# Sliding attention: two masked score blocks merged ahead of the exponent and parted behind the transpose

## The chip, the cores and the metric

The kernel runs on one NeuronCore of a Trainium2 chip. Its time is device microseconds of one execution; three runs were timed. The engines are named as in the profile: PE is TensorE's matmul, PEld its weight load, DVE is VectorE, ACT is ScalarE, POOL is GpSimd, SP is SyncE, which issues most DMAs.

## The reference

Two layers of a hybrid decoder over 256 tokens of width 1024, in float32. Each layer normalises its input, projects it once into everything that three parallel mixers need (a state-space scan called SSD, sliding-window attention, forgetting attention called fox), gates and projects the three results, merges them and adds the sum to the residual. The change lies in the sliding-window attention, 16 heads in 4 groups that share keys and values:

```python
qb = q.reshape(b, nb, blk, SWA_KV_HEADS, SWA_GROUP, HEAD_DIM)      # blk = 128, nb = 2
scores = jnp.einsum('bnqkgd,bnskd->bnkgqs', qb, kb) * (HEAD_DIM ** -0.5)
diff = qi + blk - sj                                               # sj: 0..255, own block and the one before
band = (diff >= 0) & (diff < SWA_WINDOW)                           # window 128
scores = jnp.where(mask, scores, -jnp.inf)
probs = jax.nn.softmax(jnp.concatenate([scores, sink], axis=-1), axis=-1)[..., :-1]
out = jnp.einsum('bnkgqs,bnskd->bnqkgd', probs, vb)
return out * jax.nn.silu(z)
```

The window is as long as a block. A query of the second block at place i sees the keys of its own block at places j <= i, and those of the block before at places j > i. So of the two keys with the same place j, one in each block, it sees exactly one. A query of the first block has only its own block.

## The kernel before, in words

The work is a long row of dense products on TensorE: the input projection in pieces of 256 or 512 columns, then the branch projections and the output projection. Weights come in by DMA (`raw`, issued by SyncE), ScalarE copies them to a rounded high part (`hi`, L264) and VectorE subtracts that from them for a low part (`lo`, L265). Each product takes three passes over the high and low parts (`dense`, 24 matmuls for one unit). Up to six `hi` and `lo` tiles are held.

TensorE executes in the order in which the program is written out (`tc.manual_schedule(engines={ENG.PE})`). The order on VectorE, ScalarE and GpSimd is made by the framework's scheduler from the dependences; each engine then executes its own list in order.

Small work is put between the dense products by a planner. It keeps a clock in estimated TensorE microseconds (`mm` and `transpose` add to it). A piece of small work is a generator. When it yields a number, such as `D_SOFT = 7.0`, `D_SOFT2 = 3.0` or `D_EVAC = 3.0`, it may go on at the first call of `pump` after so much of that clock; when it yields a function, it waits until that is true; when it yields the name of a token, it waits for the token. `pump` is called at the end of a dense unit, and in the middle of one with 512 columns, and enters what is due, earliest first, until 1.35 of the clock is used up. `drain` forces all work of one branch to its end ahead of the projection that needs it.

A *quad* is the attention of four query heads, in two pairs p of two heads i. `swa_quad` makes the four quads of the sliding attention in each layer, `fox_quad` the four of the forgetting attention; both run the common `attn_quad` (L528). With the one `pp` token it

- scores both query blocks b of each head (8 matmuls into 4 PSUM tiles of the 5 named `mx`): block 0 against 128 keys, block 1 against 256;
- adds the mask or bias, scales by -1/8 and takes the row minimum on VectorE (L555), into `pp`, where a head has 128 columns for block 0 and 256 for block 1;
- takes the exponent with its row sum on ScalarE (L561), adds the sink's term to the sum (L565 to L568), and multiplies by half the reciprocal on VectorE (L573, 8 per quad; the half belongs to the SiLU of the gate);
- `D_SOFT` later, transposes the three 128 by 128 blocks of each head on TensorE (L100), 12 per quad in two blocks of six that `D_SOFT2` parts; ScalarE copies each four of them to SBUF (L590);
- `D_EVAC` later, gives the token back and, when the gate is there, multiplies with the values (8 matmuls, L96, `mx<-L,L`) and with the gate on VectorE (L603).

The sliding quads run beside the projections of the gate (`u_z`), of the convolution (`u_conv`) and the values of fox (`u_cv`). The SSD groups (`ssd_group`) begin when no work of the sliding branch waits any more. GpSimd prepares the biases of the fox quads (`affine_select`, L867), adds the rotated halves of queries and keys (L492, L513) and little else. In `u_bkv`, ScalarE copies the values from PSUM to `y.bv`.

## Time and profile before

| | us |
|---|---|
| three runs: lowest, median, highest | 847.7, 848.38, 850.29 |
| span of the profiled execution, from its first to its last instruction | 846.0 |
| PE busy | 833.7 |
| PEld busy | 763.4 |
| DVE busy | 642.3 |
| ACT busy | 511.6 |
| POOL busy | 105.7 |

The page gives the profiled execution by its span; what lies around the span is not in it, and the median of the timed runs is 2.4 us above it. Busy time of an engine is the union of its instructions' spans; matmuls overlap, so the sum of their durations is larger than the busy time. In the lists of groups, a line gives the line of the kernel, engine, operation, tiles written and read, shapes and count, then the group's busy time in us and the mean duration of one in ns, then the idle time of the engine just before such instructions and what ended it. A row of the timeline gives start and length in us, then the same names. A row of the windows gives a stretch and the busy time and count of instructions of each engine in it, then the TensorE clock granted (1.00 is full), the share of the DMA engines, and GB/s. The row of one line's instructions gives the shortest, median and longest duration in ns.

### The profile page before, as it was taken

The page shows a single profiled execution, that of the slowest core. Times are in us where ns is not written, and L with a number is a line of the kernel's source. Part 1 is how long each engine was busy: PE and PEld are TensorE (multiplying, and loading weights), DVE is VectorE, ACT ScalarE, POOL GpSimd, SP SyncE. Part 2 cuts the span into 40 slices and gives each one's busy share as a digit, 9 for nine tenths or more (in the row PEclk, how much of TensorE's full clock was granted, in tenths as well). Part 3 has the DMA queues.
Part 4 walks back from the last instruction along what each step waited for, and adds up shares of the span by engine and source line. Part 5 has one row for each costly group of instructions (what it writes and reads, how often), then busy time and mean ns, then how long its engine had stood idle before and what let it go on. Part 6 is the DMA issues. An engine that isn't in the chain of part 4 may idle for free.

```text
span 846.0 us, 15985 instructions
## 1 busy us (share of the span) xinstructions
PE 833.7 (99%) x5964; PEld 763.4 (90%) x5964; DVE 642.3 (76%) x1403; ACT 511.6 (60%) x1004; POOL 105.7 (12%) x134
## 2 busy tenths in 40 slices
PE   8999999999999999999999999999999999999996
PEld 7989898998999998888989998899899999988896
DVE  5777997998776669656788879879968567785665
ACT  6466777665666667435555667776557667654442
POOL 6410100000140010210014001000003110121000
PEclk9999999999999999999999999999999999999999
DMA  9576565666465545748676465465755654576632
GB/s 303 160 226 197 180 199 163 197 212 184 143 188 177 181 145 189 230 147 292 206 237 218 144 204 157 145 200 182 239 172 176 174 175 152 161 236 211 212 100 76
DMA packets 126638, 158.43 MB, mean 187 GB/s; under 512 B 12784, under 2 KB 88224, under 8 KB 126560
## 3 DMA queue, kind: packets, MB, share of 16 engines
q1 hardware_dynamic: 109456, 140.79, 52.5%
q10 hardware_dynamic: 17056, 16.49, 6.3%
q8 instruction: 47, 0.77, 0.4%
q14 instruction: 31, 0.25, 0.1%
q0 software_dynamic: 48, 0.13, 0.0%
HBM read 155.22 MB, written 2.16 MB: 186 GB/s over the span
## 4 chain that ended last, share of the span: by engine, by line
PE 95%; DMA 3%; DVE 1%; ACT 0%; POOL 0%; issue 0%; SPq 0%; POOLq 0%; DVEq 0%
PE mm L96 82%; PE mx L96 9%; PE mx L100 4%; DMA raw<-in_w_in_dram 3%; DVE lo L265 0%; POOL lo L1154 0%; ACT hi L1153 0%; DVE L L470 0%; ACT L L1013 0%; DVE L L265 0%; ACT L L264 0%; POOLq L1218 0%; ACT L L215 0%; DVE L L996 0%; DVE L L1001 0%
## 5 line engine op out<-in xcount | busy, mean ns | idle before, releaser
L265 DVE TENSOR_TENSOR lo<-raw,hi 128x1024 fp32r<-128x1024 f32 x252 | 308.3, 1235 | 93.8 <-ACT hi L264 84.6
L96 PE MATMUL mm<-hi,L 128*128 128x512 f32 (+1 forms) x1344 | 373.9, 364 | 2.0 <-ACT hi L1153 1.5
L264 ACT ACTIVATE hi<-raw 128x1024 fp32r<-128x1024 f32 x252 | 263.4, 1056 | 93.5 <-PE mm L96 75.5
L96 PE MATMUL mm<-L,hi 128*128 128x256 f32 x1792 | 317.7, 278 | 0.7 <-DVE L L473 0.7
L96 PEld LDWEIGHTS mm<-L,hi 128*128 128x128 f32 x1792 | 277.7, 192 | 7.6 <-issue 3.3
L96 PEld LDWEIGHTS mm<-hi,L 128*128 128x128 f32 x1344 | 241.5, 190 | 32.5 <-issue 2.7
L96 PE MATMUL mm<-L,lo 128*128 128x256 f32 x896 | 246.4, 275 | 0.0
L96 PE MATMUL mm<-lo,L 128*128 128x512 f32 (+1 forms) x672 | 241.4, 361 | 0.6 <-POOL lo L1154 0.6
L96 PEld LDWEIGHTS mm<-L,lo 128*128 128x128 f32 x896 | 171.9, 192 | 0.2
L96 PEld LDWEIGHTS mm<-lo,L 128*128 128x128 f32 x672 | 127.3, 190 | 15.4 <-POOL lo L1154 0.8
L867 POOL TENSOR_SCALAR_AFFINE_SELECT bias<-bias 128x128 f32<-128x128 f32 x64 | 35.9, 597 | 407.5 <-DVE L L736 268.6
L561 ACT ACTIVATE pp<-pp,nm 128x128 f32<-128x128 f32 (+1 forms) x128 | 56.5, 443 | 13.5 <-DVE nm L555 13.5
L698 DVE SCALAR_TENSOR_TENSOR L<-L,vec,L 128x255 f32<-128x255 f32 (+2 forms) x96 | 46.3, 482 | 4.7 <-ACT L L695 3.4
L96 PE MATMUL mx<-L,L 128*64 128x128 f32 (+1 forms) x384 | 34.4, 314 | 0.0
L891 ACT ACTIVATE L<-L 128x512 f32<-128x512 f32 x24 | 15.1, 631 | 29.9 <-DVE L L890 29.7
L573 DVE TENSOR_SCALAR pp<-pp,rsum 128x128 f32<-128x128 f32 (+1 forms) x128 | 32.2, 316 | 0.5
L701 ACT ACTIVATE L<-L 128x256 f32<-128x256 f32 x32 | 13.3, 417 | 31.5 <-DVE L L698 25.9
L96 PEld LDWEIGHTS mx<-L,L 128*64 128x64 f32 x384 | 23.0, 136 | 9.4 <-ACT pp L561 1.3
L782 ACT ACTIVATE L<-mm 128x256 f32<-128x256 f32 x48 | 18.1, 378 | 20.8 <-PE mm L96 20.8
L590 ACT ACTIVATE L<-mx 128x512 f32<-128x512 f32 x48 | 27.0, 597 | 2.7 <-PE mx L100 2.5
L100 PE MATMUL mx<-ident,pp 128*128 128x128 f32 x192 | 26.3, 273 | 0.0
L555 DVE CUSTOM_DVE_ANT_0 pp<-mx,wmask,nsink 128x128 f32<-128x128 f32 x64 | 23.4, 412 | 1.5 <-PE mx L96 1.5
(173 smaller groups left out, 717.5 us busy)
## 6 DMA issues: line engine op xcount, KB each, us to landing
raw<-in_w_in_dram SPq DMA_DIRECT2D x200, 512.0 KB, 4.5
raw<-in_w_proj_dram SPq DMA_DIRECT2D x48, 512.0 KB, 5.5
raw<-in_w_out_dram SPq DMA_DIRECT2D x16, 512.0 KB, 4.6
L<-cumd ACTq DMA_DIRECT2D x8, 512.0 KB, 5.0
bias<-cumd ACTq DMA_DIRECT2D x16, 256.0 KB, 4.0
L<-in_gate_bias_dram ACTq DMA_DIRECT2D x12, 256.0 KB, 3.9
L<-in_x_dram SPq DMA_DIRECT2D x2, 512.0 KB, 4.9
nwb<-in_norm_w_dram SPq DMA_DIRECT2D x1, 512.0 KB, 5.3
```

Source lines behind the costliest of these rows:

```text
L96: nc.tensor.matmul(o, a, b, **kw)
L100: nc.tensor.transpose(o, a, i)
L264: keep(act)(hi, src, AF.Copy)
L265: keep(tt)(lo, src, hi.bitcast(F32), op=ALU.subtract)
L555: nc.vector.tensor_tensor_reduce(out=pp[:, i, sl], in0=score(p, i, b), in1=biases(p, i, b), scale=-0.125, scalar=1.0e30 if ns is None else ...
L561: act(pp[:, i, sl], pp[:, i, sl], AF.Exp, scale=-1.0, bias=nm[:, e:e + 1], accum_out=sums[:, e:e + 1])
L573: ts(pp[:, i, sl], pp[:, i, sl], rs[:, 2 * i + b:2 * i + b + 1], 0.5, op0=ALU.mult, op1=ALU.mult)
L590: act(pT, pt, AF.Copy)
L698: stt(a[:, s:S], x_[:, 0:S - s], y.vec[:, 16 * j + u:16 * j + u + 1], a[:, s:S], op0=ALU.mult, op1=ALU.add)
L782: act(halves(th), p, AF.Tanh, scale=0.5)
L867: nc.gpsimd.affine_select(out=bias[:, i, dst], in_=bias[:, i, src], compare_op=ALU.is_ge, fill=NEG, base=0, pattern=[[-1, P]], channel_mul ...
L891: act(g, g, AF.Tanh, scale=0.5)
```

## The change

`swa_quad` no longer uses `attn_quad` but has a body of its own; `fox_quad` is untouched. The score matmuls, masks and row minima stay. Then, for the second query block, VectorE takes the minimum of the two masked blocks of 128 columns. `pp` holds the negated scores, in which a masked place is very large, so the minimum keeps at each place the score of the one key that is seen. The exponent of this block runs over 128 columns. The reciprocal is multiplied in with one product for a pair, and its half moves into the values (`scale=0.5` on the copies of `y.bv`).

Each head has now two blocks to transpose, 8 per quad in two blocks of four. Behind the transpose, ScalarE copies the four blocks of a pair to `pT`, and the second query block of both heads once more to `own`. GpSimd sets to zero in `pT` the keys that belong to the query's own block, and in `own` those that belong to the block before (`affine_select`, two per pair). The matmuls with the values have the shapes they had. They come a new delay `D_SEL = 2.5` after the token is given back.

```diff
-                act(halves(y.bv[:, t, :]), p, AF.Copy)
+                act(halves(y.bv[:, t, :]), p, AF.Copy, scale=0.5)
...
+D_SEL = 2.5
...
     def swa_quad(y, c, qT):
         yield lambda: (1, 0) in y.zdone
-        yield from attn_quad(
...
+                tt(pp[:, i, P:2 * P], pp[:, i, P:2 * P], pp[:, i, 2 * P:3 * P], op=ALU.min)
+                for b in range(2):
+                    e = 4 * p + 2 * i + b
+                    sl = slice(b * P, (b + 1) * P)
+                    act(pp[:, i, sl], pp[:, i, sl], AF.Exp, scale=-1.0, bias=nm[:, e:e + 1],
+                        accum_out=sums[:, e:e + 1])
...
+            pv = pp[:, :, 0:2 * P].rearrange("p i (b k) -> p i b k", b=2)
+            s4 = [P, 2, 2, P]
+            tt(pv, pv, rs.rearrange("p (i b) -> p i b", i=2).unsqueeze(3).to_broadcast(s4), op=ALU.mult)
+        yield D_SOFT
...
+        own = T("L2", [P, 4, P])
+        prev = []
+        for p in range(2):
+            pt = pmx()
+            for i in range(2):
+                for b in range(2):
+                    transpose(pt[:, (2 * i + b) * P:(2 * i + b + 1) * P], pps[p][:, i, b * P:(b + 1) * P], ident)
+            pT = T("L2", [P, 2, 2, P])
+            p4 = pt.rearrange("p (i b q) -> p i b q", i=2, b=2)
+            act(pT, p4, AF.Copy)
+            act(own[:, 2 * p:2 * p + 2, :], p4[:, :, 1, :], AF.Copy)
+            nc.gpsimd.affine_select(out=pT[:, :, 1, :], in_=pT[:, :, 1, :], compare_op=ALU.is_ge, fill=0.0,
+                                    base=-1, pattern=[[0, 2], [-1, P]], channel_multiplier=1)
+            nc.gpsimd.affine_select(out=own[:, 2 * p:2 * p + 2, :], in_=own[:, 2 * p:2 * p + 2, :],
+                                    compare_op=ALU.is_ge, fill=0.0, base=0, pattern=[[0, 2], [1, P]],
+                                    channel_multiplier=-1)
+            prev.append(pT)
+            if p == 0:
+                yield D_SOFT2
+        yield D_EVAC
+        tokens["pp"] += 1
+        yield D_SEL
+        yield lambda: (1, 2 * c + 1) in y.zdone
...
+                    x_ = prev[p][:, i].rearrange("p b q -> p (b q)") if b == 0 else own[:, 2 * p + i, :]
+                    mm(o, y.bv[:, b, vc], x_, start=(b == 0), stop=(b == 1))
```

More of the change, by code (lines that the diff above doesn't have):

```diff
@@ L484, in f @@
             if c0 > 0:
-                act(halves(y.bv[:, t, :]), p, AF.Copy)
+                act(halves(y.bv[:, t, :]), p, AF.Copy, scale=0.5)
             elif w.n == 512:
-                act(y.bv[:, t, :], p[:, 1, :], AF.Copy)
+                act(y.bv[:, t, :], p[:, 1, :], AF.Copy, scale=0.5)
             if c0 == 0:
@@ L606, in swa_quad @@
         yield lambda: (1, 0) in y.zdone
-        yield from attn_quad(
-            [qT[:, j, :] for j in range(2)], [y.kT[:, c, :]] * 2,
-            lambda p, i, b: wmask[:, P:2 * P] if b == 0 else wmask,
-            y.nsink[:, 4 * c:4 * c + 4], y.bv, lambda p, i: slice(64 * c, 64 * c + 64),
-            lambda: y.sz[1][:, 2 * c:2 * c + 2, :], lambda: (1, 2 * c + 1) in y.zdone)
+        yield "pp"
+        pps = [T("pp", [P, 2, 3 * P]) for _ in range(2)]
+        nm = T("nm", [P, 8], bufs=2)
@@ new lines, in swa_quad, with score @@
+        sums = T("sums", [P, 8], bufs=2)
+        kT = y.kT[:, c, :]
+        scs = [pmx() for _ in range(4)]
+        def score(p, i, b):
+            return scs[2 * p + i][:, b * P:P + 2 * P * b]
+        for p in range(2):
+            for b in range(2):
+                for i in range(2):
+                    r = slice(64 * i, 64 * i + 64)
+                    mm(score(p, i, b), qT[r, p, b * P:(b + 1) * P], kT[r, 0:(b + 1) * P], start=True, stop=True)
+        for p in range(2):
+            pp = pps[p]
+            ns = y.nsink[:, 4 * c + 2 * p:4 * c + 2 * p + 2]
+            ps_ = slice(4 * p, 4 * p + 4)
+            for i in range(2):
+                for b, sl, m in ((0, slice(0, P), wmask[:, P:2 * P]), (1, slice(P, 3 * P), wmask)):
+                    e = 4 * p + 2 * i + b
+                    nc.vector.tensor_tensor_reduce(
+                        out=pp[:, i, sl], in0=score(p, i, b), in1=m, scale=-0.125, scalar=ns[:, i:i + 1],
+                        op0=ALU.add, op1=ALU.min, accum_out=nm[:, e:e + 1])
+                tt(pp[:, i, P:2 * P], pp[:, i, P:2 * P], pp[:, i, 2 * P:3 * P], op=ALU.min)
+                for b in range(2):
+                    e = 4 * p + 2 * i + b
+                    sl = slice(b * P, (b + 1) * P)
+                    act(pp[:, i, sl], pp[:, i, sl], AF.Exp, scale=-1.0, bias=nm[:, e:e + 1],
+                        accum_out=sums[:, e:e + 1])
+            es = T("es", [P, 4], bufs=2)
+            tt(es.rearrange("p (i b) -> p i b", i=2), nm[:, ps_].rearrange("p (i b) -> p i b", i=2),
+               bc(ns, 2, 2), op=ALU.subtract)
+            act(es, es, AF.Exp)
+            tt(sums[:, ps_], sums[:, ps_], es, op=ALU.add)
+            rs = T("rsum", [P, 4], bufs=4)
+            nc.vector.reciprocal(rs, sums[:, ps_])
+            pv = pp[:, :, 0:2 * P].rearrange("p i (b k) -> p i b k", b=2)
+            s4 = [P, 2, 2, P]
+            tt(pv, pv, rs.rearrange("p (i b) -> p i b", i=2).unsqueeze(3).to_broadcast(s4), op=ALU.mult)
@@ new lines, in swa_quad @@
+        yield D_SOFT
+        own = T("L2", [P, 4, P])
+        prev = []
+        for p in range(2):
+            pt = pmx()
+            for i in range(2):
+                for b in range(2):
+                    transpose(pt[:, (2 * i + b) * P:(2 * i + b + 1) * P], pps[p][:, i, b * P:(b + 1) * P], ident)
[11 more added lines that the diff above has]
+                yield D_SOFT2
@@ new lines, in swa_quad @@
+        yield D_EVAC
+        tokens["pp"] += 1
+        yield D_SEL
+        yield lambda: (1, 2 * c + 1) in y.zdone
+        sz = y.sz[1][:, 2 * c:2 * c + 2, :]
+        vc = slice(64 * c, 64 * c + 64)
+        py = pmx()
+        for p in range(2):
+            for b in range(2):
+                for i in range(2):
+                    o = py[64 * i:64 * i + 64, S * p + P * b:S * p + S]
+                    x_ = prev[p][:, i].rearrange("p b q -> p (b q)") if b == 0 else own[:, 2 * p + i, :]
+                    mm(o, y.bv[:, b, vc], x_, start=(b == 0), stop=(b == 1))
@@ L614, in u_small @@
+        tt(sz, py.rearrange("p (u s) -> p u s", u=2), sz, op=ALU.mult)
     def u_small(y):
```

## The prediction

> **What bounds the kernel now.** I read the page first: the span, the busy times, the slices, and the shares of the chain that ended last.

> ```profile
> span 846.0 us, 15985 instructions
> PE 833.7 (99%) x5964; PEld 763.4 (90%) x5964; DVE 642.3 (76%) x1403; ACT 511.6 (60%) x1004; POOL 105.7 (12%) x134
> ...
> PE   8999999999999999999999999999999999999996
> ...
> PEclk9999999999999999999999999999999999999999
> ...
> PE 95%; DMA 3%; DVE 1%; ACT 0%; POOL 0%; issue 0%; SPq 0%; POOLq 0%; DVEq 0%
> ```

> TensorE is busy in 833.7 of 846.0 us, at nine tenths in every slice but the first and the last, with the clock granted throughout, and it holds 95% of the chain. The other engines have room. So the time is the length of TensorE's instruction stream plus what that stream waits, and a change counts only as far as it shortens the one or lengthens the other.

> The sliding attention of the two layers runs between about 50 and 165 us and between about 464 and 580 us (the masked reductions with `wmask` lie there). The windows view of these two stretches shows whether TensorE has gaps there:

> ```profile
> core 0: us, PE busy (x) PEld busy (x) DVE busy (x) ACT busy (x) POOL busy (x), PEclk, DMA share, GB/s
> 50.00:165.00 115.00, 114.27 (x890) 104.36 (x889) 100.55 (x266) 82.71 (x192) 6.04 (x10) 1.00 0.61 191
> 464.00:580.00 116.00, 116.00 (x901) 106.08 (x900) 98.88 (x260) 83.25 (x193) 5.56 (x9) 1.00 0.56 176
> ```

> It has none: 114.27 of 115 us, and 116.00 of 116. VectorE has 14 to 17 us free per stretch, ScalarE over 32, GpSimd nearly all.

> **The change part by part.**

> *TensorE: 32 transposes fewer.* A quad (one group of four query heads) had 12 transposes in two blocks of six; now it has two blocks of four. Score and value matmuls keep their number and shapes: the second query block still scores 256 keys, and the values still see one product of 256 columns and one of 128 per head. There are 4 quads in each of 2 layers: 8 x 4 = 32 transposes go. The price of one is read from the length of a block, from its first start to the start of what follows:

> ```profile
> 139.51 0.82 PE L100 MATMUL mx<-ident,pp 128*128 128x128 f32 x6
> 140.09 0.46 PE L96 MATMUL mm<-hi,L 128*128 128x512 f32 x1
> ```

> ```profile
> 403.53 0.60 PE L100 MATMUL mx<-ident,L 128*128 128x128 f32 x4
> 403.89 0.47 PE L96 MATMUL mm<-hi,L 128*128 128x256 f32 x2
> ```

> Six take 140.09 - 139.51 = 0.58 us, four (another place of the same program) 0.36 us: 0.22 us per block, 0.11 per transpose. Over 16 blocks that is 16 x 0.22 = 3.5 us. The group of these transposes gives another figure, the duration of one:

> ```profile
> L100 PE MATMUL mx<-ident,pp 128*128 128x128 f32 x192 | 26.3, 273 | 0.0
> L561 ACT ACTIVATE pp<-pp,nm 128x128 f32<-128x128 f32 (+1 forms) x128 | 56.5, 443 | 13.5 <-DVE nm L555 13.5
> L573 DVE TENSOR_SCALAR pp<-pp,rsum 128x128 f32<-128x128 f32 (+1 forms) x128 | 32.2, 316 | 0.5
> L590 ACT ACTIVATE L<-mx 128x512 f32<-128x512 f32 x48 | 27.0, 597 | 2.7 <-PE mx L100 2.5
> ```

> 273 ns each would make 8.7 us, but they overlap (192 x 273 ns is 52 us, the group is busy for 26.3), so I take 0.11. The ends are 3.5 and 8.7, and the block lengths stand at the first.

> *VectorE: about even, and hidden.* The reductions over scores and mask stay. Per quad, 8 normalising multiplications (316 ns mean) become 2 tensor-by-tensor products over 512 columns, and 4 minima over 128 columns come in. The nearest rows for the new forms, and for two more below:

> ```profile
> L754 DVE TENSOR_TENSOR L<-L,mx 128x512 f32<-128x512 f32 x16 | 10.6, 682 | 1.5 <-PE mx L96 1.5
> L473 DVE TENSOR_TENSOR L<-mm,rope 128x128 f32<-128x128 f32 x20 | 5.6, 281 | 0.0
> L522 ACT ACTIVATE qt<-mx 128x256 f32<-128x256 f32 x16 | 5.3, 372 | 4.3 <-PE mx L100 4.3
> ```

> 2 x 0.68 + 4 x 0.28 = 2.5 us against 8 x 0.32 = 2.5 us. Even at half a microsecond more per quad, the 2 us per layer fit in the 14 us that VectorE has free there. If that cover were gone, 4 us would come back.

> *ScalarE: slightly less, hidden.* Four exponents per quad shrink from 256 to 128 columns:

> ```profile
> 101.21 0.40 ACT L561 ACTIVATE pp<-pp,nm 128x128 f32<-128x128 f32 x1 [0.28 <-DVE nm L555]
> ...
> 101.61 0.51 ACT L561 ACTIVATE pp<-pp,nm 128x256 f32<-128x256 f32 x1
> ```

> That saves 4 x 0.11. One evacuation of three goes (0.60) and two copies `own` of 256 columns come (2 x 0.37): together 0.3 us less per quad. The halved copy of the values costs nothing new: the scale rides on a copy that was there. The exponents now wait for the minimum as well, 0.28 us later per head. Between a quad's scores and its first transposes lie about 10 us, as on the third quad:

> ```profile
> 99.31 1.58 PE L96 MATMUL mx<-L,qt 64*128 64x128 f32 x16
> ...
> 110.43 0.82 PE L100 MATMUL mx<-ident,pp 128*128 128x128 f32 x6
> ```

> There the later exponents end long before TensorE asks for them, so nothing behind them is late.

> *GpSimd: 32 new selects, and a wait added ahead of the values.* Each quad gets four selects over 256 columns. The value matmuls cannot start before the last is done; TensorE's order is written out, so all dense matmuls behind them would stand too. What is queued on GpSimd there is the fox bias selects alone (L867), the nearest row:

> ```profile
> L867 POOL TENSOR_SCALAR_AFFINE_SELECT bias<-bias x64: 285/292/6287, 86.5 to 689.2; 128x128 f32<-128x128 f32 x64
> ```

> 292 ns at the median for 128 columns, so between 0.29 and 0.58 for 256; I take 0.58. But the longest took 6.29 us. The room for this wait, on the two tightest quads of the first layer, from the last transposes through the evacuation to the values:

> ```profile
> 93.38 0.82 PE L100 MATMUL mx<-ident,pp 128*128 128x128 f32 x6
> ...
> 103.61 0.44 PE L96 MATMUL mx<-L,L 128*64 128x256 f32 x2
> ```

> ```profile
> 96.16 0.60 ACT L590 ACTIVATE L<-mx 128x512 f32<-128x512 f32 x1
> ```

> ```profile
> 140.56 0.60 ACT L590 ACTIVATE L<-mx 128x512 f32<-128x512 f32 x1
> ```

> ```profile
> 145.44 1.52 PE L96 MATMUL mx<-L,L 128*64 128x256 f32 x16
> ```

> On the second quad the evacuation ends at 96.76 and the values start at 103.61: 6.85 us. New in it: the first select can follow at once, the copy `own` (0.37) runs beside it, two selects take 1.16. That leaves 5.7 us. On the fourth quad there are 145.44 - 141.16 = 4.3 us now, and the added delay of 2.5 on the planner's clock puts the values at the next place where the planner is called, 12 matmuls later; 24 of them lie between 140.09 and 145.44, so this is 2.7 us: 7.0 us for the same 1.2. The other quads keep their places, because there the next quad's scores already come between, and they have more. So I take the wait at nothing; its bounds are 0 and, with the longest select seen on every quad, the rival below. The `pp` token is given back ahead of the new delay, so no quad starts later; only the fourth quad's end moves by 2.7 us, and with it the start of the SSD groups, which two convolution pairs and more separate from whoever drains them.

> *What the lock-out is.* The longest select stands beside this stretch of VectorE:

> ```profile
> 230.46 7.76 POOL L867 TENSOR_SCALAR_AFFINE_SELECT bias<-bias 128x128 f32<-128x128 f32 x7 [134.89 <-DVE L L736]
> ```

> ```profile
> 231.37 2.36 DVE L265 TENSOR_TENSOR lo<-raw,hi 128x1024 fp32r<-128x1024 f32 x2
> 233.64 0.69 DVE L743 TENSOR_TENSOR L<-L,L 128x512 f32<-128x512 f32 x1
> 234.24 2.36 DVE L265 TENSOR_TENSOR lo<-raw,hi 128x1024 fp32r<-128x1024 f32 x2
> 236.51 0.41 DVE L785 SCALAR_TENSOR_TENSOR L<-L,mm 128x256 f32<-128x256 f32 x1
> ```

> Seven selects of 0.29 would be 2 us and took 7.76: the first hung until 236.7, as long as VectorE went from one instruction with two SBUF sources to the next, and ended at the first that reads PSUM (`mm`). [...]

> *The sum.* The profiled execution has a span of 846.0 us; the median of the timed runs is 848.38, 2.4 us above it, taken as unchanged. 846.0 - 3.5 = 842.5 for the span, 848.38 - 3.5 = **844.9 us** for the time.

> **The rivals.**

> *Locked out (slower).* The selects of the second head pair hang behind VectorE's splits (`lo<-raw,hi`) and the new products, which have two SBUF sources too. For: the 6.29 us; VectorE is busy for 87% of the first stretch. Against: in the stage itself ten GpSimd instructions took 6.04 us in all, and VectorE pauses or reads PSUM often. If each quad meets one such lock-out (6.3), one `lo` split more (1.2) and 1.16 of its own, the chain is 8.7 us against 6.85: 1.8 us on a tight quad. Four tight quads (two per layer) give 7.2, so 844.9 + 7.2 = 852.1 us. It decides from 0.76 us of wait per quad on, where 8 x 0.76 exceeds 3.5 + 2.5.

> *Given back in small waits (no change).* The kernel re-enters dense work 32 times after attention blocks; the order on VectorE and ScalarE is made anew by the scheduler. With 0.06 us lost at each, 2 us return: 846.9 us. For: VectorE has little air in single 10 us slices. Against: the same places show no idle TensorE now.

> *The whole duration counts (faster still).* If removing a transpose takes out its 273 ns, 8.7 us go: 839.7 us. Against it stand the block lengths.

> That the change does not do what it says concerns the exponents and the products: they get no shorter path to the end, since neither engine is on it. That is in the sum already.

> **How the numbers follow.** A difference of 0.3%, 2.5 us, is about what a measurement of this kernel can tell from no change; faster is below 845.8, slower above 850.9. Chances: the forecast 0.70, given back 0.15, locked out 0.12, the whole duration 0.03. The forecast's own spread is about 843.5 to 845.8, from waits of up to 1 us and the spread of the runs; I count all of it as faster, with the fourth case: 0.73 faster, 0.15 within, 0.12 slower. The range goes from 843.0 to 849.0 us: it holds the forecast, the small waits, and a lock-out on one or two quads; outside are the full lock-out and the whole duration.

> **What would show it.** Right: 32 fewer transposes in the group, blocks of four 0.36 us long, TensorE still without gaps in both stretches, the span about 842.5. Wrong: idle time of TensorE or its weight loads ahead of the value matmuls, released by GpSimd's select; selects of several microseconds ending where VectorE pauses; dense matmuls waiting for VectorE right after the scores. If the span falls by about 8.7 us, the pitch was the wrong price; if it falls by 3.5 and the time does not, what lies around the span has moved.

## The result and the profile after

| | before | after |
|---|---|---|
| median of 20 runs each, us | 847.78 (846.95 to 853.14) | 844.81 (843.74 to 849.21) |
| span of the profiled execution, us | 846.0 | 842.9 |

The ratio is 0.9964, with a 95% interval from 0.9953 to 0.9975: by the ratio the changed kernel is faster by 3.05 us (2.1 to 4.0); the medians differ by 2.97. Forecast were 844.9 us and a gain of 3.5. That the absolute number came out closer than the gain did is luck: the kernel before measured 847.78 in these runs and 848.38 in the three that the forecast started from.

The page of the changed kernel, with the lines that answer to those of before:

```profile
span 842.9 us, 15995 instructions
PE 829.5 (98%) x5932; PEld 758.9 (90%) x5932; DVE 641.9 (76%) x1387; ACT 509.2 (60%) x1012; POOL 125.8 (15%) x166
...
PE   7999999999999999999999999999999999999996
...
PEclk9999999999999999999999999999999999999999
...
PE 88%; DMA 5%; DVE 2%; issue 2%; ACT 1%; POOL 0%; ACTq 0%; SPq 0%; POOLq 0%; DVEq 0%
```

TensorE has 32 instructions less (5964 to 5932) and 4.2 us less busy time; the span is 3.1 us shorter. VectorE and ScalarE hardly move. GpSimd works 20 us more: 17.4 of them are the selects, and the rest its bias selects, which take a little longer (38.6 us for 35.9). The chain's share of PE fell from 95% to 88%, but TensorE is still busy for 98% of the span, so this share isn't read as time that other engines cost.

The windows of the two sliding stretches:

```profile
core 0: us, PE busy (x) PEld busy (x) DVE busy (x) ACT busy (x) POOL busy (x), PEclk, DMA share, GB/s
50.00:165.00 115.00, 114.11 (x879) 104.03 (x878) 101.34 (x259) 84.58 (x200) 16.45 (x26) 1.00 0.62 193
464.00:580.00 116.00, 116.00 (x887) 105.43 (x888) 101.02 (x256) 81.87 (x193) 14.41 (x25) 1.00 0.58 179
```

TensorE is as full as before (114.11 of 115, and 116.00 of 116), so the selects (`x26` and `x25` on POOL, where 10 and 9 stood) don't hold it up. The waits of TensorE, by who ended them (total us, times, longest), the first five of seven lines:

```profile
PE mx L101 <- POOL ident masks.py:199: 1.5, 1, 1.5
PE mm L97 <- POOL lo L1226: 1.4, 2, 0.8
PE mm L97 <- ACT hi L1225: 1.4, 1, 1.4
PE mm L97 <- DVE L L474: 0.9, 1, 0.9
PE mx L101 <- DVE L L1012: 0.7, 1, 0.7
```

No wait for a select (L662, L664) is among the seven. The timeline shows a block of transposes and the matmul behind it:

```profile
140.21 0.60 PE L101 MATMUL mx<-ident,pp 128*128 128x128 f32 x4
140.57 0.46 PE L97 MATMUL mm<-hi,L 128*128 128x512 f32 x1
...
148.51 1.52 PE L97 MATMUL mx<-L,L 128*64 128x256 f32 x16
```

Four transposes take 140.57 - 140.21 = 0.36 us, where six took 0.58. The third row is the fourth quad's value matmuls. The last selects ahead of them, on GpSimd:

```profile
141.72 0.41 POOL L662 TENSOR_SCALAR_AFFINE_SELECT L<-L 128x256 f32<-128x256 f32 x1 [4.67 <-ACT L L660]
142.08 0.41 POOL L664 TENSOR_SCALAR_AFFINE_SELECT L<-L 128x256 f32<-128x256 f32 x1
```

They end at 142.49, 6.0 us before the values start. All selects of the kernel, shortest, median and longest in ns:

```profile
L662 POOL TENSOR_SCALAR_AFFINE_SELECT L<-L x16: 408/483/1472, 66.7 to 554.2; 128x256 f32<-128x256 f32 x16
```

```profile
L664 POOL TENSOR_SCALAR_AFFINE_SELECT L<-L x16: 402/498/591, 67.4 to 554.5; 128x256 f32<-128x256 f32 x16
```

The forecast took 580 ns for each. The longest, 1.47 us at 72.40, began together with a split of VectorE (`lo<-raw,hi`, 72.39 to 73.61) and ended 0.26 us behind it: a small case of what the prediction calls a lock-out, far from 6.29.

**Where the 3 us came from.** Between the same dense matmuls in both traces (counted by number, so that nothing but what lies between differs), in us; layer 0 is matmul 230 to 2060, layer 1 is 2560 to 3400, and each contains its four quads. "_2" and "_3" are further executions, below:

```
             start     layer 0    boundary   layer 1    to the last quarter
             0-230     230-2060   2060-2560  2560-3400  3400-4735
before        42.11     314.32      95.85     147.32     228.57
before_2      41.70     313.33      97.05     147.32     228.57
before_3      41.68     313.33     100.58     147.32     228.57
after         41.65     312.74      96.65     145.57     228.57
after_2       43.71     312.86      98.16     145.57     228.57
after_3       41.58     311.80      99.48     145.57     228.56
e1_dup        41.57     313.66      97.53     147.32     228.57
e2_drop       41.77     313.09      96.74     145.57     228.57
e3_nosel      42.06     312.14      97.76     145.57     228.57
e8_no_d_sel   41.64     311.91      96.31     145.57     228.56
```

In layer 1 every execution repeats to a hundredth, and the change is worth 147.32 - 145.57 = 1.75 us: 16 transposes of 0.109. Followed from matmul to matmul, the traces part there by 0.22 us at each of the eight blocks of transposes; what else moves (the fourth quad's values and SSD work) comes back in full. In layer 0 one wait of up to 1 us behind the first quad's scores (`PE mm L97 <- DVE L L474` above) is there in some executions and not in others, of either kernel. With it, 314.32 became 312.74 and 312.86; almost without it, 313.33 became 311.80: about 1.5. From dense matmul 234 on, right behind this wait, layer 0 repeats as well: 309.39 us to 2060 in all three executions of the changed kernel and in e2, e3 and e8, 311.18, 311.18 and 311.38 in those of before, 311.13 in e1. That is 1.79 us, and with layer 1 the whole 3.5. The piece ahead of it, four dense matmuls with the first quad's scores and the wait, took 2.15 to 2.95 us in before and 2.41 to 3.47 in the changed kernel; three executions of each don't settle whether the change lengthens them. The start and the boundary between the layers, which the change doesn't touch, scatter by 2.1 and 4.7 us between executions, more than half of the whole gain or more than all of it.

**The quads moved in layer 0.** The change also moved work that the prediction left in place. The dense matmul behind which the scores of quads 2, 3 and 4 stand in layer 0, and the values of quad 4:

```
             scores of quads 2, 3, 4    values of quad 4
before         376    520    652             760
e1_dup         376    520    652             772
after          400    532    664             784
e2_drop        400    532    664             772
```

The planner's clock counts 0.109 for each transpose (`clock["t"] += 0.109` in `transpose`). With fewer of them, later work falls due at a later call of `pump`: so e1, which puts the transposes back, returns to the old places, and e2, which only takes transposes out, has the new ones. In layer 1 the quads keep their places, but for the fourth quad's values (3140 to 3152). The later places in layer 0 cost no time that shows: the stretch behind dense matmul 234 is as long as the transposes make it.

### The profile page after: what moved, and what is told of

Read it like the earlier page. It is cut to its first block, busy times and chain, and to the rows that moved or that the text cites. A ratio compares the mean times of both kernels' runs of the same rounds, so it can differ in the third digit from the quotient of the medians.

```text
span 842.9 us, 15995 instructions
## 1 busy us (share of the span) xinstructions
PE 829.5 (98%) x5932; PEld 758.9 (90%) x5932; DVE 641.9 (76%) x1387; ACT 509.2 (60%) x1012; POOL 125.8 (15%) x166
## 4 chain that ended last, share of the span: by engine, by line
PE 88%; DMA 5%; DVE 2%; issue 2%; ACT 1%; POOL 0%; ACTq 0%; SPq 0%; POOLq 0%; DVEq 0%
PE mm L97 75%; PE mx L97 9%; PE mx L101 3%; DMA raw<-in_w_in_dram 3%; DMA raw<-in_w_proj_dram 1%; DVE lo L266 1%; DMA L<-in_x_dram 1%; DVE L L1068 0%; DVE L L1091 0%; ACT hi L260 0%; ACT hi L265 0%; ACTq L260 0%; POOL sm L227 0%; ACT L L216 0%; DVE L L266 0%
## 5 line engine op out<-in xcount | busy, mean ns | idle before, releaser
L97 PE MATMUL mm<-hi,L 128*128 128x512 f32 (+1 forms) x1344 | 372.8, 363 | 1.9 <-ACT hi L1225 1.4
L97 PE MATMUL mm<-L,hi 128*128 128x256 f32 x1792 | 317.8, 278 | 0.9 <-DVE L L474 0.9
L265 ACT ACTIVATE hi<-raw 128x1024 fp32r<-128x1024 f32 x252 | 262.9, 1055 | 87.1 <-PE mm L97 59.5
L97 PEld LDWEIGHTS mm<-L,hi 128*128 128x128 f32 x1792 | 277.6, 192 | 7.9 <-issue 3.5
L97 PEld LDWEIGHTS mm<-hi,L 128*128 128x128 f32 x1344 | 241.1, 189 | 32.3 <-issue 2.4
L97 PE MATMUL mm<-L,lo 128*128 128x256 f32 x896 | 246.4, 275 | 0.0
L97 PE MATMUL mm<-lo,L 128*128 128x512 f32 (+1 forms) x672 | 241.3, 360 | 1.4 <-POOL lo L1226 1.4
L97 PEld LDWEIGHTS mm<-L,lo 128*128 128x128 f32 x896 | 171.9, 192 | 0.1
L97 PEld LDWEIGHTS mm<-lo,L 128*128 128x128 f32 x672 | 126.9, 189 | 16.4 <-POOL lo L1226 1.9
L939 POOL TENSOR_SCALAR_AFFINE_SELECT bias<-bias 128x128 f32<-128x128 f32 x64 | 38.6, 635 | 269.4 <-DMA bias<-cumd 237.7
L97 PE MATMUL mx<-L,L 128*64 128x128 f32 (+1 forms) x384 | 34.4, 314 | 0.0
L562 ACT ACTIVATE pp<-pp,nm 128x128 f32<-128x128 f32 x64 | 28.2, 443 | 6.9 <-DVE nm L556 6.9
L97 PEld LDWEIGHTS mx<-L,L 128*64 128x64 f32 x384 | 23.0, 136 | 9.4 <-issue 2.0
L637 ACT ACTIVATE pp<-pp,nm 128x128 f32<-128x128 f32 x64 | 25.1, 393 | 10.3 <-DVE nm L630 9.0
L854 ACT ACTIVATE L<-mm 128x256 f32<-128x256 f32 x48 | 18.2, 379 | 19.5 <-PE mm L97 19.4
L662 POOL TENSOR_SCALAR_AFFINE_SELECT L<-L 128x256 f32<-128x256 f32 x16 | 10.2, 639 | 114.5 <-ACT L L660 114.5
L1008 POOL TENSOR_TENSOR L<-L,L 128x512 f32<-128x512 f32 x8 | 15.9, 1995 | 57.9 <-DVE L L1007 32.1
```

What stands on the lines that cost most here:

```text
L97: nc.tensor.matmul(o, a, b, **kw)
L265: keep(act)(hi, src, AF.Copy)
L562: act(pp[:, i, sl], pp[:, i, sl], AF.Exp, scale=-1.0, bias=nm[:, e:e + 1], accum_out=sums[:, e:e + 1])
L637: act(pp[:, i, sl], pp[:, i, sl], AF.Exp, scale=-1.0, bias=nm[:, e:e + 1], accum_out=sums[:, e:e + 1])
L854: act(halves(th), p, AF.Tanh, scale=0.5)
L939: nc.gpsimd.affine_select(out=bias[:, i, dst], in_=bias[:, i, src], compare_op=ALU.is_ge, fill=NEG, base=0, pattern=[[-1, P]], channel_mul ...
```

## The experiments

The theory: the gain is the 32 transposes at their pitch, 0.11 us each, and everything else is hidden. Rivals: it comes from the shorter exponents or a better order; or part of a larger gain is given back by selects and waits.

**e1_dup: the changed kernel with its 32 transposes back.**

```diff
                 for b in range(2):
-                    transpose(pt[...], pps[p][:, i, b * P:(b + 1) * P], ident)
+                    for _ in range(1 + b):
+                        transpose(pt[...], pps[p][:, i, b * P:(b + 1) * P], ident)
```

> The changed kernel, but each transpose of a merged block is issued twice onto the same place, so that a quad has 12 transposes again; all else of the change stays. Theory (the gain is TensorE's time for 32 transposes, 0.11 us each): the 3.5 us come back, ratio to the kernel before 0.999 to 1.001 (0.8 us of a new wait at the end of layer 0 may stay). Rival (the gain comes from shorter exponents and one evacuation less on ScalarE, or from the new order of the other engines): the time stays at that of the changed kernel, ratio 0.9964.

Measured: 848.44 us beside 848.04, ratio 1.0003 [0.9987, 1.0020], span 846.4. Its group of transposes is that of before again:

```profile
L101 PE MATMUL mx<-ident,pp 128*128 128x128 f32 x192 | 26.3, 273 | 0.0
```

The whole gain is gone while the merged exponents and the selects stay, and layer 1, where TensorE's order stays that of the changed kernel too, takes 147.32 us to the hundredth. In layer 0 the quads return to their old places, so there e1 doesn't part the order from the transposes. The rival of ScalarE falls, and by layer 1 that of the order.

**e2_drop: the kernel before, only without the 32 transposes.** In the sliding quads the transposes of the second query block's own keys and the third evacuation are left out, and the value product reads another block in their place, so the result lacks these keys.

```diff
+        if merged:
+            order = [(h, b) for h in range(4) for b in range(2)]
...
-            if n == 6:
+            if n == len(order) // 2:
...
-                    n, c = at[2 * p + i, 2 * b]
+                    n, c = at[2 * p + i, b if merged else 2 * b]
```

> The kernel before, but the sliding quads leave out the transpose of the second query block's own keys (4 of 12) and the third evacuation, and use the transposed block of the earlier keys in its place in the value matmuls; no merge, no selects, no added delay. Theory: all of the gain, 3.5 us, ratio 0.9959 (0.995 to 0.997). Rival (merge and shorter exponents carry it): ratio within 0.999 to 1.001.

Measured: 845.38 us beside 848.04, ratio 0.9964 [0.9949, 0.9979], span 843.7, layer 1 at 145.57. That is the same ratio as the change's, with no merge, no selects and no longer delay. What the change adds costs nothing that shows, and its shorter exponents bring nothing.

**e3_nosel: the changed kernel without the 32 selects.**

```diff
-            nc.gpsimd.affine_select(out=pT[:, :, 1, :], ...)
-            nc.gpsimd.affine_select(out=own[:, 2 * p:2 * p + 2, :], ...)
```

> The changed kernel without GpSimd's 32 selects, so that the value matmuls see each merged block unparted. Theory (selects and their wait lie wholly beside dense matmuls): the same as the changed kernel, ratio 0.9964 within 0.001. Rival (locked out: TensorE waits for selects, or VectorE loses time to them that TensorE feels): faster than the changed kernel by over 1 us, ratio under 0.995.

Measured: 845.78 us beside 848.04, ratio 0.9975 [0.9963, 0.9987], span 843.8. The ratio lies just outside the 0.001 expected, on the slower side. Without its selects the kernel isn't faster than with them (0.9964), and its two stretches, 309.39 and 145.57 us, are those of the changed kernel to the hundredth: where the selects stand they are free.

**e4_tight and e5_tight_nosel: the cover taken away.** In the changed kernel the values now come right behind the evacuation, so that the chain from the transposes to the values lies bare, and the token comes back only behind them; e5 is the same without the selects.

```diff
-        yield D_EVAC
-        tokens["pp"] += 1
-        yield D_SEL
...
         tt(sz, py.rearrange("p (u s) -> p u s", u=2), sz, op=ALU.mult)
+        tokens["pp"] += 1
```

> The changed kernel with the delays between transposes and values taken out (no D_EVAC, no D_SEL, token given back after the values): TensorE comes to the value matmuls right behind the last transposes and must wait out evacuation, copy and both selects. Theory (the delays cover a chain of about 2.5 to 5 us per quad): slower than before by 8 x 3 to 5 less 3.5 us, so 865 to 885 us. Rival (the chain is short and the delays cover nothing that matters): within 2 us of the changed kernel. Rival locked out: single waits of over 6 us, above 890 us.

> As the kernel with the delays taken out, but without the 32 selects: TensorE waits out evacuation and copy alone. Theory (the selects are a real but hidden part of the chain, about 1 us per quad, and what a pause of TensorE costs grows with its length): 8 to 15 us faster than the 874.75 us with selects, so 860 to 867 us, with fewer stretches at a granted clock of 0.50. Rival (the wait is evacuation, and selects add nothing): within 3 us of 874.75.

Measured: e4 874.75 us beside 848.04, ratio 1.0320 [1.0296, 1.0343], span 871.9; e5 861.24 beside 847.73, ratio 1.0166 [1.0144, 1.0188], span 860.6. Of each, the first line of TensorE's waits, e4 first:

```profile
PE mx L97 <- POOL L L662: 17.8, 8, 4.1
```

```profile
PE mx L97 <- ACT L L660: 10.8, 8, 4.5
```

TensorE now waits once in each of the eight quads, and with the selects 7.0 us longer in all than for the evacuation alone: 0.9 us per quad in the mean (in one of them the wait was longer without), where the forecast had put 1.16 for two selects. But the spans differ by 11.3 us, not 7. The windows of e4 behind its pause at 97.7 to 101.8 show why:

```profile
core 0: us, PE busy (x) PEld busy (x) DVE busy (x) ACT busy (x) POOL busy (x), PEclk, DMA share, GB/s
98.00:100.00 2.00, 0.00 (x0) 0.00 (x0) 1.93 (x5) 0.98 (x3) 0.00 (x0) 1.00 0.84 175
100.00:102.00 2.00, 0.20 (x2) 0.20 (x4) 2.00 (x5) 2.00 (x6) 0.68 (x2) 1.00 1.03 382
102.00:103.00 1.00, 1.00 (x9) 0.34 (x5) 0.52 (x2) 0.92 (x3) 0.28 (x1) 0.58 0.97 315
103.00:104.00 1.00, 1.00 (x5) 0.82 (x4) 0.92 (x2) 0.07 (x1) 0.00 (x0) 0.50 1.05 390
104.00:105.00 1.00, 1.00 (x4) 0.82 (x3) 1.00 (x2) 0.00 (x0) 0.00 (x0) 0.50 0.96 327
105.00:106.00 1.00, 1.00 (x5) 0.85 (x4) 0.24 (x1) 0.00 (x0) 0.43 (x2) 0.72 0.43 142
106.00:107.00 1.00, 1.00 (x6) 0.61 (x4) 0.00 (x0) 0.00 (x0) 1.00 (x5) 1.00 0.82 146
```

TensorE stands from 98 to nearly 102, and then the granted clock is 0.50 from 102.2 to 105.6: 3.4 us in which TensorE is fully "busy" and does half the work. The first two dense matmuls of 512 columns behind the values take 1.01 us from start to start (102.97 to 103.98), where those of the same quad in the kernel before take 0.53 (105.06 to 105.59). So another 1.7 us are lost, an estimate from the 3.4 us and the clock. Pauses are counted here from one matmul's start to the next one's, less the usual 0.06 us; the view of the waits, which goes by modelled ends, has 0.2 less. In e4 four of the eight pauses at the values have a halved clock behind them (those of 4.31, 4.04, 2.48 and 2.42 us), and none of the others (2.20, 1.98, 1.04, 1.04); in e5 two (4.70 and 2.84 us), and none up to 1.09. Behind the pause of 4.70 it lasted 6.83 us, from 97.9 to 104.7, and TensorE was back at 99.0: some 2.8 us lost. So e4's 29.0 us over the changed kernel are 19.5 of pauses at the values, 4 x 1.7 = 6.8 of halved clock and 2.8 at the layer boundary, where executions of one kernel differ by as much; e5's 17.7 are 12.5, 2.8 + 1.7 = 4.5, and 0.7 at the boundary. The delays that the prediction counted as cover are worth 26 us in the quads of e4, and the selects inside them 9.4 there; the whole spans differ by 29.0 and 11.3.

**e8_no_d_sel: the changed kernel without the added delay.**

```diff
-D_SEL = 2.5
+D_SEL = 0.0
```

> The changed kernel with D_SEL = 0, so that only the fourth quad's value matmuls come earlier, by half a dense unit. Theory (6 us of room there, of which the selects need about one): the same time as the changed kernel, ratio 0.9964 within 0.001, and no idle TensorE ahead of the values. Rival locked out: a wait of 1 us or more on one of the two fourth quads, ratio over 0.9975.

Measured: 845.82 us beside 847.73, ratio 0.9977 [0.9967, 0.9988], span 841.6. The fourth quad's values come 24 dense matmuls behind their transposes again, as before the change, and not 36:

```profile
139.22 0.60 PE L101 MATMUL mx<-ident,pp 128*128 128x128 f32 x4
144.93 1.52 PE L97 MATMUL mx<-L,L 128*64 128x256 f32 x16
```

There is still no wait ahead of them: the last select ends at 141.49, 3.4 us before. The span is the shortest of all profiled executions, while the ratio missed what was expected (0.9964 within 0.001) and passed the 0.9975 that was to mark a lock-out. But a lock-out was to show as a wait of 1 us or more, and there is none; the two stretches are those of the changed kernel (309.39 and 145.57 us), and the intervals of the two ratios overlap: no difference that can be told. The added delay isn't needed in these runs, and isn't paid for either.

**e6_dm: the wait at the layer boundary.** In the changed kernel's profile the transposes of the merged branches wait 0.7 us for VectorE (L1012), in that of before nothing. Was this the missing half microsecond, brought by the change?

```diff
-D_GN1, D_GN2, D_CUM, D_H, D_M = 4.0, 6.0, 12.0, (4.8, 7.0), 5.0
+D_GN1, D_GN2, D_CUM, D_H, D_M = 4.0, 6.0, 12.0, (4.8, 7.0), 5.3
```

> The changed kernel with D_M = 5.3 in place of 5.0, so that the transposes of the merged branches come half a dense unit later in both layers. Theory (0.9 us of the 3.5 are given back where TensorE waits for VectorE's merge at the end of layer 0, at 385 us of the changed kernel's profile): that wait goes, 0.5 to 0.9 us faster than the changed kernel, ratio 0.9954 (0.9945 to 0.996). Rival (the gap between 3.5 and the measured 3.05 is the spread of the runs): ratio 0.9964 as for the changed kernel.

Measured: 845.62 us beside 847.73, ratio 0.9975 [0.9965, 0.9985], span 844.7. A miss, and no test: the longer delay moved only the other block of these transposes (from dense matmul 2128 to 2140); the one that waits stayed at 2152, and it waited 1.3 us.

**before_2, before_3, after_2, after_3: both kernels again, unchanged.** These take up the question of e6 again.

> The kernel before, unchanged, for a second profile. The wait of TensorE at the end of layer 0 (transposes of the merged branches behind VectorE's merge), 0.9 us in the changed kernel's profile and absent in the first profile of before: if it belongs to the change, this profile has none either; if it belongs to the phase of the single execution, this or the next profile has one of 0.3 to 1.5 us.

> As the run before it: a third profile of the kernel before, for the same question.

> The changed kernel, unchanged, for a second profile. If the wait at the end of layer 0 belongs to the change, 0.9 us again; if to the phase of the single execution, another size. The matmul stream of the two stretches with sliding attention: without a wait ahead of the values in either case, 3.5 us shorter than in before.

> As the run before it: a third profile of the changed kernel, for the same question.

Measured, one execution each, span and time: before_2 845.6 and 847.33, before_3 849.5 and 851.17, after_2 846.6 and 848.57, after_3 844.8 and 846.47. The boundary's wait in the kernel before (before_3), and in the changed one (after_3), each the first of TensorE's waits:

```profile
PE mx L100 <- DVE L L940: 2.5, 1, 2.5
```

```profile
PE mx L101 <- DVE L L1012: 2.6, 1, 2.6
```

Counted from start to start, as above, it is 0.10, 1.31 and 2.71 us in the three executions of before, and 0.87, 1.76 and 2.73 in those of the changed kernel. Each kernel has it short and long, so it goes with the single execution; that the change adds nothing to it is not shown by three of each. What sets it in an execution wasn't found. DMA shares near 1.0 stand around it (1.04 and 1.05 from 384 to 392 us in before_3), but also in the first execution of before (1.05 and 1.07 from 380 to 388 us), which has no such wait.

## Why the prediction was right, point by point

- **The bound.** Right: TensorE is full in both stretches in both kernels. As long as the delays cover the rest, only its instructions moved the time (e1, e2, e3).
- **The transposes, 3.5 us.** Right in count (32) and in price. Layer 1 gives 0.109 us each, and blocks of four are 0.36 us long. e1 takes the gain back with transposes alone, e2 gets it with transposes alone. The interval of the measured 3.05 us (2.1 to 4.0) holds 3.5, and the traces give 1.75 and 1.79 us in the stretches with the blocks. Whether a part of it is given back at the first quad's scores, as the measured middle would have it, stays open.
- **VectorE and ScalarE hidden.** Right: no wait of TensorE is put down to the minima, the products or the copies, and e2, without any of them, has the same ratio. Even the sums came: VectorE's busy time is level (642.3 and 641.9 us), ScalarE's 2.4 us less, which is 8 x 0.3.
- **GpSimd's selects at no cost.** Right in the sum; the size was somewhat high: 0.58 us was taken for each, and the medians are 0.48 and 0.50 (1.47 at most). Ahead of the fourth quad's values 7.0 us less 1.2 were forecast as room, and 6.0 were left. e4 and e5 show that it is this room that makes them free: without it TensorE waits 17.8 us with the selects and 10.8 without.
- **The moved fourth quad.** Its values came at 148.51, where 145.44 + 2.7 = 148.1 was worked out. That is partly luck: they moved by 24 dense matmuls (760 to 784), 12 by the added delay as worked out and 12 with the whole quad, while the shorter blocks and a different start took time off. The prediction didn't say whether the delay was needed; without it 4.3 us were enough (e8).
- **"The other quads keep their places", "no quad starts later".** Wrong in layer 0, right in layer 1. In layer 0 the second quad starts 24 dense matmuls later and the third and fourth 12. It did no harm: TensorE stayed full, and no wait stands ahead of the values. The sum had nothing in it for such a move, so that it cost nothing was not foreseen but lucky.
- **The surroundings of the span, taken as unchanged.** The span fell by 3.1 us, the median by 2.97.
- **Locked out.** It didn't happen in the sliding stretches: the longest select there is a quarter of the 6.29 us that the rival took. The lock-out itself is still in this kernel, outside these stretches and beside the same chain of VectorE instructions. It doesn't look like a chance event: the first profile of either kernel has exactly two, one per layer, of 6.29 and 6.26 us in before (at 230.46 and 643.89) and of 6.04 and 5.89 in the changed kernel (at 228.44 and 641.04), and each of the four ends 0.23 to 0.24 us behind the start of the first VectorE instruction of this chain that reads `mm`. Why a select hangs there no run shows. The longer of them in the changed kernel:

```profile
L939 POOL TENSOR_SCALAR_AFFINE_SELECT bias<-bias x64: 288/294/6040, 90.1 to 686.2; 128x128 f32<-128x128 f32 x64
```

  The rival's price was too low in one respect. It counted a wait at its own length; in e4 four pauses from 2.42 us on cost about 1.7 us more.
- **Given back in small waits.** Not seen in the stretches with the blocks, which are shorter by all of the 3.5 us. The waits elsewhere that differ between the two first profiles are no more than what two executions of one kernel differ by.
- **The whole duration counts.** Wrong, as weighed: 16 x 0.273 would have been 4.4 us in layer 1, and 1.75 came.

## What to carry to other kernels

Where one engine that works in order is full, a change is worth that engine's instructions that it removes, each at its pitch (from start to start, here 0.109 us) and not at its duration (here 0.273); measure this between the same two instructions of both traces, which was exact to 0.01 us here while the whole span scattered by 4. Work that is moved to another engine was free here as long as the room between the last producer and the consumer was longer than the new chain (the selects ahead of the fourth quad's values ended 6.0 us before them, and 3.4 in e8, with no wait), so look for that room in the timeline before looking at the engine's busy share. And a pause of the bounding engine can cost more than its length (here by 1.7 us five times and by 2.8 once). Where a planner places work by an estimated clock, taking instructions out also moves what comes behind them; compare the places before calling the rest unchanged.

## What the hardware showed that was not expected

```profile
384.00:388.00 4.00, 2.55 (x11) 1.58 (x9) 3.56 (x4) 2.89 (x4) 0.00 (x0) 1.00 1.04 369
388.00:392.00 4.00, 2.73 (x10) 2.34 (x11) 3.11 (x5) 1.14 (x3) 0.00 (x0) 0.75 1.05 351
392.00:396.00 4.00, 4.00 (x17) 3.31 (x17) 2.06 (x2) 2.72 (x3) 0.00 (x0) 0.83 0.28 84
```

  Pauses as short as 2.42 us brought it (e4). The length of the pause alone doesn't decide: 2.71 us brought it in before_3, and 2.73 us at the same place in after_3 didn't. In e4 and in the first profile of before the halved stretches begin whole multiples of 3.4133 us apart (e4 at 74.85 us and 8, 133 and 146 times that later; before at 13.10 us and 243 times that later, at 842.53), as the windows of a fixed grid would; that there is such a grid is a reading of these starts. Two windows of this grid in e4, each with the next one behind it; the first holds most of a pause of 2.53 us at the layer boundary, the second that of 2.48 us at the last quad's values:

```profile
core 0: us, PE busy (x) PEld busy (x) DVE busy (x) ACT busy (x) POOL busy (x), PEclk, DMA share, GB/s
399.11:402.52 3.41, 1.47 (x9) 1.36 (x10) 3.23 (x6) 0.92 (x3) 0.00 (x0) 1.00 1.06 356
402.52:405.93 3.41, 3.41 (x18) 2.98 (x17) 2.44 (x3) 2.93 (x4) 0.00 (x0) 1.00 0.53 195
569.78:573.19 3.41, 1.36 (x13) 0.80 (x11) 3.30 (x3) 2.72 (x5) 0.89 (x1) 1.00 0.72 178
573.19:576.60 3.41, 3.20 (x16) 2.49 (x17) 0.69 (x1) 0.00 (x0) 0.52 (x2) 0.50 0.99 263
```

  TensorE was idle for 1.94 us of the first window and for 2.05 of the second. In the first profiles of before and of the changed kernel, from 20 us to 8 us before the end, no window of the grid has more than 0.73 us of idle time, and none is halved. In the first 20 us, with other work, less was enough (1.62 us in before, from 9.68 to 13.09, with the clock at 0.50 from 13.10 to 16.51), so idle time alone doesn't decide either.
- **Scatter with a place.** The executions of one kernel differ by up to 4 us of span, and most of it lies at two places, the start (41.6 to 43.7 us) and the layer boundary (95.9 to 100.6), while the stretch of layer 1 repeats to 0.01 us.
